# Gate products of an encoder block: reordered first products, splits on GpSimd, earlier tiles for the merge

## The chip, the cores and the metric

The kernel runs on one core of a Trainium2 chip. The metric is device time in microseconds of one execution. The engines are TensorE (PE; its weight loads are PEld), VectorE (DVE), ScalarE (ACT), GpSimd (POOL) and SyncE (SP), which here only issues transfers. Each engine takes its instructions in order.

## The reference

The input is 1024 tokens of width 1024, with 16 meta tokens in front. One layer is computed:

```python
h = h + mixer_block(rms_norm(h, norm_mix), ...)
h = h + swiglu(rms_norm(h, norm_ffn), w_ff_gate, w_ff_up, w_ff_down)
return rms_norm(h, norm_final)[:, N_META:]
# mixer_block: proj = h @ w_in, cut into qa, ka, va, qb, kb, vb, ga, gb
y_a = differential_attention(qa, ka, va, ...)   # 4 heads, every key, two softmaxes subtracted
y_b = windowed_gqa(qb, kb, vb, sink)            # 8 heads, window of 128, meta tokens and sinks
merged = sigmoid(ga) * (y_a @ w_ba) + sigmoid(gb) * (y_b @ w_bb)
return merged @ w_o
```

All of it is float32. The gates ga and gb are 1024 wide each, so their projections are a 1024 x 1024 by 1024 x 2048 product.

## The kernel before

**Precision.** A float32 operand is split in two fp32r tiles, high and low: the high part is a rounded copy, the low part the remainder. A product is three fp32r matmuls: high x high, high x low, low x high. `split` (line 118) makes the copy on ScalarE (line 119) and subtracts on the engine that its last argument names (line 120).

**Stages.** In order: normalisation and projections with the windowed attention (to about 295 us); the differential attention of four heads with the gate products filled in between (to 638 us); the merge, which multiplies both branches with w_bb and w_ba and weighs them with the gates (to 735 us); then the product with w_o and the feed-forward block. TensorE's order is written by hand inside the stages (`tc.manual_schedule`); the order on the other engines and on the queues comes from a planner that simulates a timeline, within the dependences. `tc.issue_after(x)` makes what it holds follow x.

**The gate products.** They use a two by two block scheme with seven products per pair of column blocks instead of eight (the numbers 1 to 7 are names; 1 and 2 give one block, 6 and the sums on it the others). Eight pairs k, each with two blocks of 128 columns. A product (k, p) is 12 matmuls of 128 x 128 by 512, issued in four steps of three; `fill(n)` issues n steps. Its right side (`RIGHT_G`, line 800) is a quarter of the tokens, hT_hi and hT_lo at (d, t): d the half of the width, t the half of the tokens. Some products need sums of token quarters. Those were computed earlier and lie in DRAM as t_d[0] to t_d[3], 2 MB each (high and low); `turn_into(i)` (line 804) loads t_d[i] over a quarter of hT once its last reader is done. `LAST_T` (line 801) names the product after which each is loaded; t_d[2] is loaded with the first head.

**Order.** `first_g` (line 732) holds 24 products: for two pairs at a time (k, 1), (k+1, 1), (k, 2), (k+1, 2), then (k, 6) for all eight pairs. After them come 5, 7, 3, 4 of each pair. The raw weights are read once for 1 and 2 ("f", one tile of 512 KB per pair), again for 6 ("m", two tiles) and again for the rest ("s", two tiles): 40 loads. At most four raw tiles are loaded and not yet freed, two tagged "w" in wpool and two tagged "w2" in gstage (`load_g`, line 745). `weights_g` (line 759) forms the sums of weights on GpSimd and splits the result: the copy on ScalarE, the subtraction on GpSimd. There are four tiles for split operands, so they are made up to four products ahead. The result of (k, 1) goes to DRAM as u_d[k] (line 855), is read back and added to that of (k, 6) (line 862), stored again, and read once more for products 5, 7, 3 and 4.

**Attention and fill.** `load_a` (line 895) loads the queries and keys of a head: for m = 1 and then m = 0, the queries (line 901), and the keys in three transfers (lines 902 and 904). Their tiles have one buffer each, so they wait for the last scores of the head before. Then come 24 gate steps (first head) or 6 (the others), `G_FIRST` and `G_HEAD`, and eight tiles of 128 queries, each of which issues 5 gate steps between its scores (line 934), transposes (line 963) and value products (line 976): 46 steps in a later head, 64 in the first. At the end, `HOLD` = 22 steps follow the last tile.

**The merge.** After the attention, `bops` takes space of the closed apool; the raw y_b is loaded into it. When all gate products are issued, ypool is opened, the gate pools are closed, and ybpool is opened: four tiles yb, split on ScalarE and VectorE (line 1145). The first product of the merge (line 722) reads them. Branch b uses eight weight tiles wbhb, branch a eight wbha, all from six buffers tagged "wh" (`WB_BUFS`, `branch_w` at line 711). The order of branch a keeps up to six of them in use. Gate tiles "gt" have four buffers.

## Time and profile before

| What | us |
|---|---|
| Median of three runs | 1451.18 |
| Lowest and highest run | 1450.22 and 1454.14 |
| Profiled execution | 1455.2 |
| Its span, first to last instruction | 1453.4 |
| TensorE busy in it | 1413.3 (97%) |
| VectorE busy | 914.0 (63%) |
| ScalarE busy | 702.2 (48%) |
| GpSimd busy | 604.3 (42%) |
| Transfers | 229.30 MB, mean 158 GB/s |

In the profile, L848 is line 848 of the kernel before, and names such as `pg` or `wopg` are tiles with their numbers left out: `pg` is a gate product's bank, `wopg` its split weights, `aps` the scores, `apt` the transposes, `at` their copies, `aq` and `ak` queries and keys, `ppa` the merge's products. An arrow `out<-in` gives the tiles written and read; x counts instructions. "Idle before" is the time in which an engine stood still before an instruction, with the one that released it. The granted clock is that of TensorE, 1.00 being full speed. In the slices, the span is cut in 40 equal parts of 36.3 us, and each digit is a share in tenths.

### The profile page before, as it was taken

The page shows a single profiled execution, that of the slowest core. Times are in us where ns is not written, and L with a number is a line of the kernel's source. Part 1 is how long each engine was busy: PE and PEld are TensorE (multiplying, and loading weights), DVE is VectorE, ACT ScalarE, POOL GpSimd, SP SyncE. Part 2 cuts the span into 40 slices and gives each one's busy share as a digit, 9 for nine tenths or more (in the row PEclk, how much of TensorE's full clock was granted, in tenths as well). Part 3 has the DMA queues.
Part 4 walks back from the last instruction along what each step waited for, and adds up shares of the span by engine and source line. Part 5 has one row for each costly group of instructions (what it writes and reads, how often), then busy time and mean ns, then how long its engine had stood idle before and what let it go on. Part 6 is the DMA issues. An engine that isn't in the chain of part 4 may idle for free.

```text
span 1453.4 us, 20758 instructions
## 1 busy us (share of the span) xinstructions
PE 1413.3 (97%) x7183; PEld 1210.1 (83%) x7183; DVE 914.0 (63%) x1584; ACT 702.2 (48%) x1340; POOL 604.3 (42%) x591
## 2 busy tenths in 40 slices
PE   9999999989789999989999999999999999999998
PEld 8998999978678888868888888888888888888886
DVE  6555666527568777734977876654555443787666
ACT  6365556536446565554445654333333333444444
POOL 4157865325367555331422134454454442000442
PEclk9999999999999999999999999999999999999999
DMA  7445564395986545177351633432232322964333
GB/s 228 91 132 160 151 199 140 95 283 184 320 253 196 183 131 183 44 264 229 112 207 58 185 105 117 138 131 102 96 108 102 102 97 99 335 216 138 129 124 145
DMA packets 197258, 229.30 MB, mean 158 GB/s; under 512 B 17480, under 2 KB 129552, under 8 KB 197152
## 3 DMA queue, kind: packets, MB, share of 16 engines
q1 hardware_dynamic: 195232, 225.13, 48.4%
q10 hardware_dynamic: 1920, 2.83, 0.6%
q8 instruction: 57, 0.93, 0.3%
q14 instruction: 49, 0.40, 0.1%
HBM read 154.84 MB, written 66.52 MB: 152 GB/s over the span
## 4 chain that ended last, share of the span: by engine, by line
PE 83%; DMA 6%; DVE 4%; SPq 2%; issue 2%; ACT 1%; POOL 1%; ACTq 0%; DVEq 0%; POOLq 0%
PE pg L1569 29%; PE pd L1673 14%; PE pg L848 6%; PE ppa L722 5%; PE po L1472 4%; PE pp_va L230 3%; PE pp_qa L230 3%; PE aps L934 3%; PE pp_ka L230 3%; PE apy L976 3%; PE bps L397 2%; PE apt L963 2%; PE pp_qb L230 2%; PE po L1480 2%; PE bpy L437 1%
## 5 line engine op out<-in xcount | busy, mean ns | idle before, releaser
L1569 PE MATMUL pg<-t,wop 128*128 128x512 f32 x1056 | 242.4, 389 | 0.0
L1569 PEld LDWEIGHTS pg<-t,wop 128*128 128x128 f32 x1056 | 198.2, 188 | 41.2
L120 POOL TENSOR_TENSOR wop<-wf,wop 128x512 fp32r<-128x512 f32 x114 | 151.3, 1328 | 163.8 <-ACT wop L119 153.6
L1673 PE MATMUL pd<-ob,oa 128*128 128x512 f32 x924 | 209.6, 389 | 0.0
L1673 PEld LDWEIGHTS pd<-ob,oa 128*128 128x128 f32 x924 | 173.4, 188 | 36.0
L1569 PE MATMUL pg<-b,wop 128*128 128x512 f32 x792 | 183.3, 389 | 0.0
L848 PE MATMUL pg<-hT_hi,wopg 128*128 128x512 f32 x448 | 173.7, 408 | 3.0 <-ACT wopg L119 2.4
L1569 PEld LDWEIGHTS pg<-b,wop 128*128 128x128 f32 x792 | 148.4, 188 | 30.7
L119 ACT ACTIVATE wop<-wf 128x512 fp32r<-128x512 f32 x128 | 80.8, 632 | 71.9 <-PE pg L1569 50.8
L120 POOL TENSOR_TENSOR oa<-ra,oa 128x512 fp32r<-128x512 f32 x27 | 34.9, 1294 | 168.6 <-ACT oa L119 167.2
L119 ACT ACTIVATE oa<-ra 128x512 fp32r<-128x512 f32 x77 | 48.7, 632 | 108.5 <-PE pd L1673 47.6
L934 PE MATMUL aps<-ak,aq 128*128 128x352 f32 (+1 forms) x384 | 88.7, 339 | 12.1 <-DMA ak<-ka_d 6.3
L848 PEld LDWEIGHTS pg<-hT_hi,wopg 128*128 128x128 f32 x448 | 86.2, 193 | 16.6 <-ACT wopg L119 2.8
L937 DVE CUSTOM_DVE_ANT_0 as<-aps,dist,far_a 128x704 f32<-128x704 f32 x64 | 60.4, 944 | 59.9 <-PE aps L934 59.8
L945 ACT ACTIVATE as<-as,amn 128x1040 f32<-128x1040 f32 x64 | 74.4, 1162 | 47.3 <-DVE amn L941 47.1
L848 PE MATMUL pg<-hT_lo,wopg 128*128 128x512 f32 x224 | 89.8, 401 | 0.0
L1346 DVE TENSOR_TENSOR s<-wf,wf 128x512 f32<-128x512 f32 x22 | 16.0, 728 | 112.0 <-DMA wf<-in_w_ff_up_dram 70.2
L934 PEld LDWEIGHTS aps<-ak,aq 128*128 128x128 f32 x384 | 65.3, 192 | 22.9 <-DMA ak<-ka_d 6.8
L399 DVE CUSTOM_DVE_ANT_0 bs<-bps,tbx,nsink 128x432 f32<-128x432 f32 (+1 forms) x64 | 38.5, 627 | 56.1 <-PE bps L397 34.6
L409 POOL TENSOR_SCALAR bs<-bs,bdn 128x432 f32<-128x432 f32 (+1 forms) x64 | 36.9, 595 | 78.2 <-DVE bdn L407 49.0
L966 ACT ACTIVATE at<-apt 128x512 fp32r<-128x512 f32 (+1 forms) x96 | 45.5, 484 | 42.1 <-PE apt L963 41.7
L976 PEld LDWEIGHTS apy<-at,av 128*128 128x128 f32 x400 | 56.0, 196 | 4.3
(318 smaller groups left out, 3139.6 us busy)
## 6 DMA issues: line engine op xcount, KB each, us to landing
ra<-aop SPq DMA_DIRECT2D x77, 256.0 KB, 2.6
wf<-in_w_ff_gate_dram SPq DMA_DIRECT2D x25, 512.0 KB, 3.6
wf<-in_w_ff_up_dram SPq DMA_DIRECT2D x25, 512.0 KB, 3.6
aop<-as SPq DMA_DIRECT2D x44, 256.0 KB, 2.1
w_c<-in_w_in_dram SPq DMA_DIRECT2D x17, 512.0 KB, 4.9
aop<-c SPq DMA_DIRECT2D x33, 256.0 KB, 2.0
t_d<-tst SPq DMA_DIRECT2D x16, 512.0 KB, 3.9
g_d<-g SPq DMA_DIRECT2D x32, 256.0 KB, 3.3
```

The costliest lines, as they stand in the source:

```text
L119: high = nc.scalar.activation(hi, src, AF.Copy)
L120: lo_eng.tensor_tensor(lo, src, f32(hi), ALU.subtract)
L230: product = nc.tensor.matmul(ps[:, :n], a[:, c, :], b[:, c, at:at + n], start=(u == 0), stop=(u == 3 * DC - 1))
L722: nc.tensor.matmul(ps, w[:, a, j, :], src(j, b, tk), start=(j == 0 and n == 0), stop=(j == 3 and n == 2))
L848: nc.tensor.matmul(ps, op[:, x, c, :], h[:, 4 * d + c, HALF[t]], start=(p in (1, 6, 7) and c == 0 and i == 0), stop=(p in (2, 6, 3, 4) and ...
L934: nc.tensor.matmul(ps[:, :n], qs[m][:, t * P:(t + 1) * P], ks[m][:, vv, k0:k0 + n], start=(vv == 0), stop=(vv == 1))
L937: nc.vector.tensor_tensor_reduce(s[m][:, 0:2 * n].rearrange("p (a k) -> p a k", a=2), two[:, :, :n], dist[:, u0:u0 + 2 * n].rearrange("p ( ...
L945: nc.scalar.activation(s[m][:, 0:L], s[m][:, 0:L], AF.Exp, bias=mn[:, m, 1:2], scale=-1.0, accum_out=dn[:, 1:2] if m else first_sum)
L976: nc.tensor.matmul(py[:, cols], v[:kp, a, k, :], at_[:kp, k, b, :], start=(k == 0 and j == 0), stop=(k == 8))
L1472: nc.tensor.matmul(sets_o[p][u], oa[:, a, u * P:(u + 1) * P], ob[:, b, :], start=(p in (1, 5) and j == 0 and k == 0), stop=(p in (2, 3) an ...
L1569: nc.tensor.matmul(ps, op[:, x, c, :], b[:, y, c, :], start=(p in (1, 5) and c == 0 and n == 0), stop=(p in (4, 2, 3) and c == 3 and n == ...
L1673: nc.tensor.matmul(ps[u], oa[:, a, u * P:(u + 1) * P], ob[:, b, :], start=(p in (1, 2, 5) and j == 0 and k == 0), stop=(p in (2, 3, 4) and ...
```

## The change

- Pairs 0 to 3 keep their order for products 1 and 2. For k = 4, 5, 6 the order is now (k, 1), (k, 6), (k, 2), (k - 4, 6); then (7, 1), (7, 6), (3, 6), (7, 2). The 24 products stay the same ones. For pairs 4 to 7 both raw tiles are loaded once and serve 1, 6 and 2, so 36 raw loads take the place of 40.
- For pairs 4 to 7 the result of product 1 stays in SBUF until product 6 adds to it; it is neither stored nor read back. For pair 7 it is copied by ScalarE into the bank of product (7, 2), which then adds to it.
- turn_into(0) follows (7, 1), turn_into(1) follows (3, 6), turn_into(3) follows (7, 2); the one that loads in four parts is now 1 and not 3.
- The gates' weights are copied and subtracted on GpSimd; ScalarE has no part in them.
- The queries of a head are loaded after the fourth raw weight.
- "w2", "s" and "ysq" move from gstage into a new pool gwork, inside gstage on the right side.
- ypool is opened before the last gate products; the first two branch weights are split and the first two gate tiles and two yb tiles opened there. When all gate weights are made, gwork is closed and the other two yb tiles are opened.
- WB_BUFS is 3. Branch a's weights 2, 3 and 4 have a tag of their own (wh2, three buffers) in yapool, which is opened when branch b is done.

```diff
 GT_BUFS = 4
-WB_BUFS = 6
+WB_BUFS = 3
 G_HEAD = 6
...
-    def branch_w(p, o, src, nme, raw=None, low=None):
+    def branch_w(p, o, src, nme, raw=None, low=None, tag="wh"):
         w = (raw_tile(f"wbr{nme}_{o}")[:, 0:512] if raw is None else raw).rearrange("p (c n) -> p c n", n=P)
...
             nc.sync.dma_start(w, src[:, o * P:(o + 1) * P].rearrange("(c p) n -> p c n", p=P))
-        wh = p.tile([P, 2, 4, P], F32R, tag="wh", name=f"wbh{nme}_{o}", bufs=WB_BUFS)
+        wh = p.tile([P, 2, 4, P], F32R, tag=tag, name=f"wbh{nme}_{o}", bufs=WB_BUFS)
         split(wh[:, 0], wh[:, 1], w, low or nc.gpsimd)
...
     gstage, close_stage = pool("gstage", "right")
+    gwork, close_gwork = pool("gwork", "right")
     apool, close_apool = pool("apool")
...
     G_COLS = [C_GB + 2 * k * P for k in range(4)] + [C_GA + 2 * k * P for k in range(4)]
-    first_g = [(k, p) for i in (0, 2, 4, 6) for p in (1, 2) for k in (i, i + 1)] + [(k, 6) for k in range(8)]
+    first_g = [(k, p) for i in (0, 2) for p in (1, 2) for k in (i, i + 1)]
+    first_g += [kp for k in (4, 5, 6) for kp in ((k, 1), (k, 6), (k, 2), (k - 4, 6))] + [(7, 1), (7, 6), (3, 6), (7, 2)]
     order_g = first_g + [(k, p) for k in range(8) for p in (5, 7, 3, 4)]
...
         else:
-            uses_g.append({1: [("f", k, 0)], 2: [], 6: [("m", k, 0), ("m", k, 1)]}[p])
+            uses_g.append({1: [("f", k, 0)], 2: [], 6: [("f", k, 1)] if k >= 4 else [("m", k, 0), ("m", k, 1)]}[p])
     loads_g = [u for us in uses_g for u in us]
...
             kind, k, i = key = loads_g[n_loaded[0]]
-            p, tag = ((wpool, "w"), (gstage, "w2"))[n_loaded[0] // 2 % 2]
+            p, tag = ((wpool, "w"), (gwork, "w2"))[n_loaded[0] // 2 % 2]
             n_loaded[0] += 1
...
                     after.enter_context(tc.issue_after(keys_a[0].ins))
-                nc.sync.dma_start(w, w_in[:, col:col + P].rearrange("(c p) n -> p c n", p=P))
-
-    sums_g, keys_a = {}, []
+                raws_g.append(nc.sync.dma_start(w, w_in[:, col:col + P].rearrange("(c p) n -> p c n", p=P)))
+
+    sums_g, keys_a, raws_g = {}, [], []
...
         nm = f"{k}_{p}"
-        kind = "s" if n >= n_first else "m" if p == 6 else "f"
+        kind = "s" if n >= n_first else "m" if p == 6 and k < 4 else "f"
         wa, wb = raw_g[kind, k, 0], raw_g.get((kind, k, 1))
...
             src = a12
-            n_freed[0] += 1
+            n_freed[0] += 1 if k < 4 else 2 if k < 7 else 4
         elif p == 6:
...
             src = a21
-            n_freed[0] += 2
+            if k < 3:
+                n_freed[0] += 2
         elif p == 5:
-            src = sums_g[k] = gstage.tile([P, 4, P], F32, tag="s", name=f"s1g_{k}", bufs=1)
+            src = sums_g[k] = gwork.tile([P, 4, P], F32, tag="s", name=f"s1g_{k}", bufs=1)
             tt(src, a21, a22, ALU.add)
...
         op = ops_g[n] = wpool.tile([P, 2, 4, P], F32R, tag=("wh", "wl")[n % 2], name=f"wopg_{nm}", bufs=W_BUFS)
-        split(op[:, 0], op[:, 1], src, nc.gpsimd)
+        nc.gpsimd.tensor_copy(op[:, 0], src)
+        tt(op[:, 1], src, f32(op[:, 0]), ALU.subtract)
...
     RIGHT_G = {1: (0, 0), 6: (0, 1), 2: (1, 0), 5: (0, 0), 7: (0, 1), 3: (1, 1), 4: (1, 0)}
-    LAST_T = {(7, 1): 0, (7, 2): 3, (7, 6): 1}
+    LAST_T = {(7, 1): (0,), (3, 6): (1,), (7, 2): (3,)}
     INTO_T = {2: (0, 1), 0: (0, 0), 1: (0, 1), 3: (1, 0)}
...
         d, t = INTO_T[i]
-        for c in (range(4) if i == 3 else (slice(0, 4),)):
+        for c in (range(4) if i == 1 else (slice(0, 4),)):
             for hl, h in enumerate((hT_hi, hT_lo)):
...
             ensure_g(n + 1)
-            for k_next in [0] * (n in (n_first - 9, n_first - 2)) + [k + 1] * (p == 6 and k < 7):
+            k_next = {(7, 6): 0}.get((k, p), k - 4 if p == 1 and k >= 4 else k + 1 if p == 7 and k < 7 else None)
+            if k_next is not None:
                 kept[k_next] = kept_g(f"u_{k_next}")
                 nc.sync.dma_start(kept[k_next], u_d[k_next])
+            if (k, p) == (3, 6):
+                banks[1, 7] = bank(psum2, f"pp{(n + 1) % 2}", "pg_7_2", 1)
+                nc.scalar.copy(banks[1, 7], kept.pop("p1"))
             if n == n_first - 1 or (p == 4 and k < 7):
...
             if p in (1, 2):
-                banks[1, k] = banks.get((1, k), banks[1])
+                banks[1, k] = banks.get((1, k), banks.get(1))
             ps = banks[1, k] if p in (1, 2) else banks[{3: 5, 4: 7}.get(p, p)]
...
                         nc.scalar.copy(p1, ps)
-                        nc.sync.dma_start(u_d[k], p1)
+                        if k < 4:
+                            nc.sync.dma_start(u_d[k], p1)
+                        else:
+                            kept[k if k < 7 else "p1"] = p1
                     elif p == 2:
...
                     elif p == 6:
-                        u = kept.pop(k)
-                        add(u, ps, u, ALU.add)
+                        p1 = kept.pop(k) if k < 7 else kept["p1"]
+                        u = p1 if k < 7 else kept_g("u_7")
+                        add(u, ps, p1, ALU.add)
                         nc.sync.dma_start(u_d[k], u)
...
                         store(st, 2 * k + (p == 4), int(p == 3))
-                    if (k, p) in LAST_T:
-                        turn_into(LAST_T[k, p])
+                    for i in LAST_T.get((k, p), ()):
+                        turn_into(i)
                     if p == 4:
                         del kept[k]
-                    if p == 7 and k < 7:
-                        kept[k + 1] = kept_g(f"u_{k + 1}")
-                        nc.sync.dma_start(kept[k + 1], u_d[k + 1])
                 yield
...
             k = ks[m] = p.tile([P, 2, L], F32R, tag=f"k{m}", name=f"ak{h}_{m}")
-            nc.sync.dma_start(f32(q), qa_d[h][m])
+            with tc.issue_after(raws_g[3].ins):
+                nc.sync.dma_start(f32(q), qa_d[h][m])
             nc.sync.dma_start(f32(k)[:, 0, :], ka_d[h][m])
...
         nm = f"{h}_{c}"
-        ysq = gstage.tile([P, 512], F32, tag="ysq", name=f"ysq_{nm}", bufs=1)
+        ysq = gwork.tile([P, 512], F32, tag="ysq", name=f"ysq_{nm}", bufs=1)
         nc.scalar.activation(ysq, py, AF.Square)
...
             nc.sync.dma_start((a12, w11)[h][:, j], yb_d[j][:, h * 512:h * 512 + 512])
+    ypool, close_ypool = pool("ypool")
+    first_w = [branch_w(ypool, o, w_bb, "b", raw) for o, raw in enumerate((a11[:, 2], asum[:, 0]))]
+
+    def gate_tile(name):
+        return ypool.tile([P, 512], F32, tag="gt", name=name, bufs=GT_BUFS)
+
+    first_gt = [gate_tile(f"gt_0_{o}") for o in range(2)]
+    yb_t = []
+
+    def split_yb(p, j0):
+        for j in (j0, j0 + 1):
+            yb_t.append(p.tile([P, 2, S], F32R, name=f"yb{j}"))
+        for h in range(2):
+            cols = slice(h * 512, h * 512 + 512)
+            for k in (j0, j0 + 1):
+                split(yb_t[k][:, 0, cols], yb_t[k][:, 1, cols], (a12, w11)[h][:, k], nc.vector)
+
+    ybpool, close_yb = pool("ybpool")
+    split_yb(ybpool, 0)
     while tail:
...
         fill(1)
+    while n_made[0] < len(order_g):
+        fill(1)
+    close_gwork()
+    ybpool2, close_yb2 = pool("ybpool2")
+    split_yb(ybpool2, 2)
     order_pe.__exit__(None, None, None)
     fill(1000)
-    ypool, close_ypool = pool("ypool")
     close_psum2()
...
     w12, w21 = (wopool.tile([P, 4, 512], F32, name=f"w{n}") for n in ("12", "21"))
-    ybpool, close_yb = pool("ybpool")
-
-    first_w = [branch_w(ypool, o, w_bb, "b", raw) for o, raw in enumerate((a11[:, 2], asum[:, 0]))]
-
-    yb_t = []
-    for j in range(4):
-        yb_t.append(ybpool.tile([P, 2, S], F32R, name=f"yb{j}"))
-        if j % 2:
-            for h in range(2):
-                cols = slice(h * 512, h * 512 + 512)
-                for k in (j - 1, j):
-                    split(yb_t[k][:, 0, cols], yb_t[k][:, 1, cols], (a12, w11)[h][:, k], nc.vector)
-
     def yb(j, b, tk):
...
         tk = slice(half * 512, half * 512 + 512)
-        gt = ypool.tile([P, 512], F32, tag="gt", name=f"gt_{i}_{o}_{half}", bufs=GT_BUFS)
+        gt = first_gt.pop(0) if first_gt else gate_tile(f"gt_{i}_{o}_{half}")
         nc.sync.dma_start(gt, g_d[8 * i + o][:, tk])
...
             split_ya(0, j)
+    close_yb2()
     close_yb()
...
         if o_next not in ws_a:
-            ws_a[o_next] = branch_w(ypool, o_next, w_ba, "a", None, nc.vector)
+            ws_a[o_next] = branch_w(*((yapool, o_next, w_ba, "a", None, nc.vector, "wh2") if 2 <= o_next < 5 else
+                                      (ypool, o_next, w_ba, "a", None, nc.vector)))
         nc.gpsimd.tensor_tensor(merged(o, half), gt, merged(o, half), ALU.add)
```

## The prediction

> **What bounds the kernel now.** I read the page's busy shares first, then the slices, then the waits of TensorE, then the single gaps in order of time, and last the queues behind them.
>
> ```profile
> span 1453.4 us, 20758 instructions
> PE 1413.3 (97%) x7183; PEld 1210.1 (83%) x7183; DVE 914.0 (63%) x1584; ACT 702.2 (48%) x1340; POOL 604.3 (42%) x591
> ...
> POOL 4157865325367555331422134454454442000442
> PEclk9999999999999999999999999999999999999999
> DMA  7445564395986545177351633432232322964333
> ```
>
> TensorE is busy for 1413.3 of 1453.4 us. The change removes no matmul (24 first products and 32 later ones, as before), so it can win only where TensorE stands still or runs slowly. Those places are in the waits of TensorE between 285 and 660 us, the gate products with the differential attention, and the start of the merge (in us: total, times, longest):
>
> ```profile
> PE aps L934 <- DMA ak<-ka_d: 6.3, 2, 4.8
> PE ppa L722 <- ACT yb L119: 6.2, 1, 6.2
> PE apt L963 <- DVE at L967: 4.7, 5, 2.0
> PE apt L963 <- DVE as L951: 3.2, 4, 1.3
> PE aps L934 <- issue: 2.7, 1, 2.7
> PE pg L848 <- ACT wopg L119: 2.4, 1, 2.4
> PE aps L934 <- DVE at L967: 1.4, 1, 1.4
> ```
>
> The same gaps in order of time (start, duration, and in brackets the idle time before):
>
> ```profile
> 295.53 0.39 PE L848 MATMUL pg<-hT_hi,wopg 128*128 128x512 f32 x1
> ...
> 306.21 0.39 PE L848 MATMUL pg<-hT_hi,wopg 128*128 128x512 f32 x1
> 309.01 0.80 PE L848 MATMUL pg<-hT_hi,wopg 128*128 128x512 f32 x1 [2.41 <-ACT wopg L119]
> ...
> 394.24 1.25 PE L934 MATMUL aps<-ak,aq 128*128 128x352 f32 x3 [4.79 <-DMA ak<-ka_d]
> ...
> 434.13 0.63 PE L963 MATMUL apt<-ident,as 128*128 128x128 f32 x4 [2.00 <-DVE at L967]
> ...
> 644.49 20.78 PE L722 MATMUL ppa<-yb,wbhb 128*128 128x512 f32 x78 [6.17 <-ACT yb L119]
> ```
>
> Behind each long gap the granted clock drops, which the table by stretch shows (us; busy time and count of PE, PEld, DVE, ACT, POOL; clock; DMA share; GB/s):
>
> ```profile
> 309.00:316.00 7.00, 6.86 (x16) 5.03 (x17) 0.00 (x0) 2.70 (x5) 4.98 (x4) 0.53 1.03 290
> 395.00:400.00 5.00, 4.64 (x23) 3.98 (x22) 2.39 (x6) 1.58 (x3) 0.00 (x0) 0.75 1.06 276
> 404.00:409.00 5.00, 5.00 (x24) 4.50 (x23) 2.98 (x7) 1.85 (x3) 3.18 (x4) 0.66 0.86 270
> 434.00:440.00 6.00, 5.87 (x28) 5.51 (x29) 5.76 (x10) 2.94 (x7) 6.00 (x6) 0.72 0.76 230
> 644.50:650.70 6.20, 6.19 (x15) 4.52 (x16) 6.20 (x12) 6.18 (x12) 0.46 (x1) 0.55 1.02 336
> 691.00:731.00 40.00, 39.80 (x176) 32.65 (x175) 39.17 (x48) 16.75 (x29) 20.18 (x12) 1.00 0.39 133
> ```
>
> A gap costs its idle time plus the busy time behind it times one minus the clock. Start of the gates: 2.4 + 6.86 x 0.47 = 5.6 us. Second head: 2.7 + 4.8 + 1.4 + 1.5 = 10.4, plus 4.64 x 0.25 + 5.00 x 0.34 = 2.9, is 13.3 us. At 434: 2.0 + 5.87 x 0.28 = 3.6 us. Merge: 6.2 + 6.19 x 0.45 = 9.0 us. Together 31.5 us: that is what the change can win, beside about 6 us of short waits on VectorE (the rest of 4.7, and 3.2).
>
> [...]
>
> **The change part by part.**
>
> *The second head's keys.* What SP issues there:
>
> ```profile
> 376.08 2.96 SPq L901 DMA_DIRECT2D aq<-qa_d  x1
> ...
> 379.61 0.38 SPq L813 DMA_DIRECT2D hT_hi<-t_d  x1
> ...
> 389.98 0.32 SPq L813 DMA_DIRECT2D hT_lo<-t_d  x1
> ...
> 391.64 0.32 SPq L901 DMA_DIRECT2D aq<-qa_d  x1
> ```
>
> The token sums of turn_into(0) and turn_into(3), 2 MB each, stand before and between the queries and keys, and the second query load goes out 15.6 us after the first, behind the last of the sums, which wait for their product on TensorE. The change fires turn_into(0) after (7, 1), turn_into(1) after (3, 6) and turn_into(3) after (7, 2), now entries 20, 22 and 23 of the order. The first head takes 24 + 8 x 5 = 64 quarter-product steps, or 16 products, so all three fall inside the second head. Also gone by then: four of 40 weight loads of 512 KB, and four stores and four loads of 256 KB (first products of pairs 4 to 7 stay on chip): 4 MB of traffic. How a head starts without sums in the way is shown by the third, which waited 0 us for keys:
>
> ```profile
> 465.00 0.32 SPq L901 DMA_DIRECT2D aq<-qa_d  x1
> ...
> 475.88 0.80 PE L934 MATMUL aps<-ak,aq 128*128 128x352 f32 x4
> ```
>
> First load to first score is 10.9 us there; in the second head TensorE stopped at 394.24 - 4.79 - 0.4 - 2.7 = 386.3, 10.3 us after 376.08, so there was as much lead. So nearly all of 13.3 us goes; I leave 1.3 (the `at` wait has another cause) and take 12.0, bounds 4 (only the 15.6 us hole in the loads closes, DMA stays full) to 13.3.
>
> *The start.* Queries and keys now follow the fourth raw weight (raws_g[3]). Now they go the other way:
>
> ```profile
> 299.17 0.55 SPq L901 DMA_DIRECT2D aq<-qa_d  x1
> ...
> 300.80 1.36 SPq L755 DMA_DIRECT2D wg_f<-in_w_in_dram  x2
> ```
>
> With the weights first, 1 MB at the 290 GB/s of that stretch lands near 299.2 + 3.6 + 2 = 305, before TensorE runs out at 306.4; the 5.6 us goes. What is late next: a step is three matmuls, 3 x (306.21 - 295.53) / 47 = 0.68 us, so 24 steps end at 311.8 and the other scores of the first tile come some 2.4 us later, at 314.2. Weights, queries and keys are 4.2 MB, 14.5 us at 290 GB/s, so the last key lands near 316. I let 2.4 us return: gain 3.2, bounds 0 to 5.6.
>
> *Gate weights on GpSimd alone.* 56 copies leave ScalarE and come to GpSimd. The rows (ns min/median/max):
>
> ```profile
> L927 POOL COPY far_m<-dist x32: 441/452/1505, 299.3 to 595.2; 128x320 f32<-128x320 f32 x32
> L952 POOL COPY as<-as x32: 199/209/220, 327.1 to 616.5; 128x32 f32<-128x32 f32 x32
> L120 POOL TENSOR_TENSOR wopg<-wg_s,wopg x24: 1271/1289/2353, 441.1 to 629.5; 128x512 fp32r<-128x512 f32 x24
> L951 DVE SCALAR_TENSOR_TENSOR as<-as,adn,as x32: 1285/1302/2386, 325.7 to 615.0; 128x1040 f32<-128x1040 f32 x32
> 432.14 0.63 ACT L119 ACTIVATE wopg<-s1g 128x512 fp32r<-128x512 f32 x1 [5.05 <-POOL s1g L781]
> ```
>
> A copy 512 wide isn't shown: bounds 0.45 (320 wide) and 1.29 (the two-input form of that width). From 32 to 320 columns it grows by 0.84 ns a column, so I take 0.61 us, nearest to the lower row. 56 x 0.61 = 34 us over 340 us is one tenth more in GpSimd slices that stand at two to seven tenths: hidden, since weights are made four products ahead and an operand takes 0.61 + 1.29 = 1.9 us against 2.7 us of a product with nothing between; a sum for product 3 or 6 adds 2.6, covered by the attention between products. If that cover is gone (1.29 a copy) a product with two sums costs 4 x 1.29 = 5.2 us against (465.00 - 376.08) / 11.5 = 7.7 us a product in the mixed stage, where a head has 46 steps or 11.5 products: still hidden. What it wins is the row at 432.14: ScalarE, in order, stood 5.05 us for a GpSimd sum with the `at` copies of the attention behind it, and the gap at 434 followed. That wait moves into GpSimd's own order: 3.6 us, bounds 0 to 3.6.
>
> The row that speaks against it is L951, two operands in SBUF: median 1.30, up to 2.39 us. One tenth more GpSimd work meets some three more of 32, and waits of up to a copy reach the short waits on VectorE: I charge 1.3 us, bounds 0 to 4. [...]
>
> *The merge's start.* The eight ScalarE halves of yb run at 643.83, all after the last gate product (ends 638.3), and TensorE waits for them:
>
> ```profile
> 643.83 4.25 ACT L119 ACTIVATE yb<-m 128x512 fp32r<-128x512 f32 x8
> ```
>
> Their data came much earlier, as the chain in order of time says (start, duration):
>
> ```profile
> 626.77 6.58 DMA m<-yb_d
> ```
>
> In the code their tiles lie in a pool opened after the gate pools close. Now ypool and the first two yb tiles lie in space that apool leaves, the other two where gwork was, free once the last weight is made, up to four products of 2.7 us or 11 us before the end. Data at 633.4 and the last four halves, 2.1 us on ScalarE and as much on VectorE behind it, fit before 638.3. What is late next: PSUM's first bank and the gates' last evacuation, under 1 us. Gain 8.0, bounds 2 (four splits after the end) to 9.0.
>
> *Fewer branch-weight buffers.* Six to three, and three more (wh2) where yb lay, so branch a's weights 2 to 4 can't be split before branch b ends: three VectorE splits move into the stretch where VectorE is busy 39.17 of 40 us. There one came just in time:
>
> ```profile
> 712.79 0.68 DVE L120 TENSOR_TENSOR wbha<-wbra,wbha 128x512 fp32r<-128x512 f32 x1
> ```
>
> 3 x 0.68 = 2.0 us of lateness there would stop TensorE for up to that, with a half clock behind it 5 us; VectorE has caught up before the next stage. I charge 1.5, bounds 0 to 5.
>
> *The rest.* Prefetches of u, seeding (7, 2) by a ScalarE copy (0.6 us, a product earlier), and the raw slots held longer: covered by one product each, bounds -1 to 1, taken as 0. The sums read later have 8 to 12 steps of 1.9 us, 15 to 23 us, before product 7, 4 or 5 reads them, against 7.2 us for 2 MB at 290 GB/s; behind SP's wait for their product stand weight loads made four products ahead: 0.
>
> **Sum.** 12.0 + 3.2 + 3.6 + 8.0 - 1.3 - 1.5 = 24.0 us. The profiled execution took 1455.2 us, 4.0 over the median of the runs: 1431.2 there, 1427 as a median.
>
> **The rivals.**
>
> *Keys still late* (0.13): SP's order puts the doubled raw loads of pairs 4 to 6 before the second head's keys. For it: DMA is full whatever moves there (share 1.06); against: 4 MB less, sums gone. The hole closes for 4 us, which the raw loads take again: 1427 + 12 = 1439.
>
> *Merge gap stays* (0.10): ScalarE or VectorE, in order, waits for another load ahead of the yb halves. For it: today they stand behind other splits; against: their data are in at 633.4. 1427 + 7 = 1434.
>
> *GpSimd blocks VectorE* (0.05): every one of the 32 L951 waits for a whole copy, 32 x 0.61 = 19.5 us on TensorE's path, 1446. For it: the 2.39 us of the row; against: the median of 1.30. [...]
>
> *Sums late* (0.08), the other side: SP's in-order queue holds turn_into(0), (1), (3) until their products end, three times 2 MB inside the second head, beside weights and u. If products 5, 7 and 4 of pair 0 each wait the full 7.2 us plus about 2.2 of half clock, 28 us is lost, and the gain of 24.0 is overtaken from three full waits on: 1427 + 28 = 1455. For it: SP waits today at 389.98; against: 15 to 23 us of lead.
>
> *All of it* (0.08): the gaps close whole and the short waits shrink with ScalarE's relief: 31.5 + 4 won, 1455.2 - 35.5 - 4.0 = 1416.
>
> **How the numbers follow.** My forecast has 0.56 (the rivals' chances taken from 1), its own range 1420 to 1434. The range 1419 to 1442 holds it and the first two rivals, and leaves out the last three, 0.21, less what of them falls short of their full price. A measurement of this kernel can tell 0.3%, 4.4 us: below 1446.8 is faster. That takes in all but the late sums, most of the blocking, and a tenth of the keys: faster 0.87, same 0.04, slower 0.09.
>
> **What would show it.** The wait of L934 for ak gone at the second head, with the reads of t_d behind it; no half clock near 310, 434 or the merge; ScalarE's L119 on wopg gone, GpSimd copies near 0.61 us; yb halves before the last gate product; wbha in the 40 us stretch later by about 2 us. I would be wrong if L848 waits for t_d or GpSimd, or if the keys still wait.

## The result, and the profile after

The changed kernel took 1431.88 us (median of 4 runs, 1430.95 to 1433.72) against 1450.7 us of the kernel before on the same chip (4 runs, 1449.28 to 1454.14): a ratio of 0.9868, 95% interval 0.9848 to 0.9889. Another series gave 1434.52 us and 0.9865 (0.9849 to 0.9882). So it is faster by about 19 us, and the predicted 1427 us was 5 us too low. The profiled execution took 1431.73 us, and its span is 23.4 us shorter than that of the profile before, which lay 4 us above its median.

The page of the changed kernel, its span and busy shares, then the slices of GpSimd, the clock and the transfers:

```profile
span 1430.0 us, 20687 instructions
PE 1406.6 (98%) x7183; PEld 1206.1 (84%) x7183; DVE 917.9 (64%) x1584; ACT 673.3 (47%) x1285; POOL 639.7 (45%) x647
...
POOL 4156865437568666332503045455444552000442
PEclk9999999999999999999999999999999999999999
DMA  8445564387687354197331724423332332954434
```

ScalarE lost 29 us of work and GpSimd gained 35: the 56 copies. TensorE's busy time fell by 6.7 us with the same 7183 matmuls, as the mean granted clock rose from 0.990 to 0.996. What TensorE waited for between 285 and 660 us (total, times, longest):

```profile
PE pg L856 <- POOL wopg L797: 5.9, 3, 3.3
PE aps L944 <- DVE amn L947: 2.5, 8, 0.4
PE aps L944 <- DMA ak<-ka_d: 2.4, 2, 1.8
PE apt L973 <- DVE as L961: 1.8, 2, 1.3
PE apt L973 <- DVE at L977: 1.4, 2, 0.7
PE ppa L722 <- ACT g L886: 0.2, 1, 0.2
```

The wait of 6.2 us at the merge and the 4.8 us for the second head's keys are gone. (The 2.4 us for keys here are the first head's.) At the top stands a wait of which the kernel before had 0.5 us: gate matmuls (L856) for the low half that GpSimd subtracts (L797). TensorE's single gaps in order of time (start, duration, in brackets the idle time before):

```profile
305.41 0.72 PE L856 MATMUL pg<-hT_hi,wopg 128*128 128x512 f32 x2 [1.04 <-POOL wopg L797]
313.64 0.40 PE L944 MATMUL aps<-ak,aq 128*128 128x352 f32 x1 [0.61 <-DMA ak<-ka_d]
315.88 1.02 PE L944 MATMUL aps<-ak,aq 128*128 128x352 f32 x3 [1.83 <-DMA ak<-ka_d]
324.20 0.66 PE L973 MATMUL apt<-ident,as 128*128 128x128 f32 x4 [1.32 <-DVE as L961]
330.51 0.80 PE L856 MATMUL pg<-hT_hi,wopg 128*128 128x512 f32 x1 [3.33 <-POOL wopg L797]
340.47 0.50 PE L856 MATMUL pg<-hT_hi,wopg 128*128 128x512 f32 x1 [1.54 <-POOL wopg L797]
...
389.13 0.80 PE L944 MATMUL aps<-ak,aq 128*128 128x352 f32 x4
...
623.75 16.62 PE L722 MATMUL ppa<-yb,wbhb 128*128 128x512 f32 x72 [0.23 <-ACT g L886]
```

The second head (389.13) starts without a gap and the merge (623.75) with 0.23 us, but the two gaps of 3.33 and 1.54 us stand where no step of the prediction had put a loss. The stretches around them (busy time and count of PE, PEld, DVE, ACT, POOL; clock; DMA share; GB/s):

```profile
316.00:320.00 4.00, 4.00 (x13) 3.42 (x14) 1.61 (x5) 0.12 (x1) 0.45 (x1) 0.57 1.05 396
...
328.00:332.00 4.00, 1.49 (x6) 1.30 (x7) 1.53 (x2) 1.74 (x3) 4.00 (x5) 0.72 1.09 347
332.00:336.00 4.00, 4.00 (x13) 3.31 (x13) 2.78 (x5) 0.88 (x2) 4.00 (x4) 0.50 0.70 254
...
667.40:707.40 40.00, 40.00 (x177) 32.97 (x176) 38.52 (x47) 16.49 (x29) 19.80 (x12) 1.00 0.50 154
```

In the stretch that holds most of the gap of 3.33 us transfers stand at 1.09; in the 4 us behind it TensorE runs at 0.50 and transfers fall to 0.70. GpSimd is busy throughout both. Why the low half is late, the rows of the changed kernel say: first two raw loads on SP's queue and what stands between them, then GpSimd:

```profile
314.35 0.39 SPq L757 DMA_DIRECT2D wg_f<-in_w_in_dram  x1
315.80 5.13 SPq L864 DMA_DIRECT2D u_d<-p  x1
321.03 0.38 SPq L757 DMA_DIRECT2D wg_f<-in_w_in_dram  x1
...
325.78 1.17 POOL L796 CAST wopg<-wg_f 128x512 fp32r<-128x512 f32 x2 [5.92 <-DMA wg_f<-in_w_in_dram]
327.97 1.26 POOL L777 TENSOR_TENSOR wg_f<-wg_f 128x512 f32<-128x512 f32 x1 [1.02 <-DMA wg_f<-in_w_in_dram]
329.19 1.27 POOL L797 TENSOR_TENSOR wopg<-wg_f,wopg 128x512 fp32r<-128x512 f32 x1
```

The first raw of pair 4 is asked for at 314.35 and used at 325.78, 11.4 us later, behind a full queue of transfers (a share of 1.05 from 310 to 320 us and of 1.06 from 320 to 330). GpSimd then makes the copies, which are the high halves, of (4, 1) and (4, 2), and next in its order stands the sum for (4, 6), which waits 1.02 us for the second raw. Only after it comes the subtraction for (4, 1), for which TensorE stands. The second raw went out late because SP stood 5.13 us on a store of u whose product wasn't done. That stand is not new: the kernel before has one of 5.22 us at 317.34. New is what hangs on the raw behind it, two sums on GpSimd.

A table from both traces and from those of the experiments below says where each stage gained. Gate product n starts with its first matmul (the gates have 12 each, so product 8 starts with the 97th), "gates' end" is the start of the last gate matmul; all lengths in us. In the names, "p_only" and so on are the runs of the next section.

| kernel | span start to product 8 | 8 to 12 | 12 to 16 | 16 to 24 | 24 to gates' end | gates' end to branch a | branch a to end |
|---|---|---|---|---|---|---|---|
| before | 329.25 | 25.31 | 27.40 | 65.95 | 190.03 | 53.01 | 762.47 |
| p_only | 328.72 | 27.12 | 26.27 | 64.41 | 189.81 | 52.80 | 762.91 |
| s_only | 325.58 | 25.00 | 27.44 | 61.46 | 190.34 | 52.29 | 762.80 |
| m_only | 328.67 | 25.31 | 27.49 | 60.77 | 192.76 | 43.79 | 762.35 |
| after | 326.45 | 32.21 | 26.28 | 47.93 | 190.27 | 44.27 | 762.55 |
| after_again | 329.19 | 32.53 | 26.30 | 48.93 | 191.66 | 43.79 | 761.99 |
| no_p | 328.31 | 30.61 | 26.28 | 52.59 | 189.98 | 43.79 | 762.17 |
| no_raws_first | 326.43 | 33.00 | 26.29 | 49.12 | 191.03 | 43.75 | 761.92 |
| sub_first | 327.57 | 32.78 | 26.29 | 47.98 | 190.31 | 44.00 | 761.99 |
| t2_late | 330.56 | 27.01 | 27.41 | 51.38 | 190.31 | 44.53 | 761.94 |
| t2_sub_first | 327.00 | 28.19 | 26.31 | 50.48 | 190.22 | 43.89 | 761.95 |
| t2_sub_again | 330.07 | 28.69 | 26.30 | 51.04 | 189.82 | 44.78 | 761.89 |
| t2_sub_hyb | 327.36 | 26.08 | 26.30 | 51.33 | 191.46 | 44.30 | 761.96 |
| no_t2 | 329.62 | 25.09 | 27.26 | 48.00 | 189.62 | 44.59 | 761.98 |

Between after and before: 18.0 us are won from product 16 to 24 (the second head), 8.7 at the merge, 6.9 are lost from product 8 to 12. Up to product 8 the three kernels that send the first queries ahead of the raw weights (before, p_only, s_only) lie at 325.6 to 329.3 and the eleven that send the raws first at 326.4 to 330.6: the profiles of one order lie as far apart as the two orders do, so the 2.8 us there can be put down to no part of the change. A row is one execution, and the profile before was one of the slower ones; after and after_again, the same kernel twice, differ by up to 2.7 us in one stage.

### The profile page after: what moved, and what is told of

Same layout as the page of the kernel before. It is cut to its first block, busy times and chain, and to the rows that moved or that the text cites. A ratio compares the mean times of both kernels' runs of the same rounds, so it can differ in the third digit from the quotient of the medians.

```text
span 1430.0 us, 20687 instructions
## 1 busy us (share of the span) xinstructions
PE 1406.6 (98%) x7183; PEld 1206.1 (84%) x7183; DVE 917.9 (64%) x1584; ACT 673.3 (47%) x1285; POOL 639.7 (45%) x647
## 3 DMA queue, kind: packets, MB, share of 16 engines
q1 hardware_dynamic: 189920, 220.94, 48.9%
## 4 chain that ended last, share of the span: by engine, by line
PE 88%; DVE 4%; DMA 4%; ACT 2%; issue 1%; SPq 1%; POOL 1%; ACTq 0%; DVEq 0%; POOLq 0%
PE pg L1591 29%; PE pd L1695 14%; PE ppa L722 6%; PE pg L856 6%; PE po L1494 4%; PE pp_va L230 3%; PE pp_qb L230 3%; PE aps L944 3%; PE pp_qa L230 3%; PE pp_ka L230 3%; PE apy L986 3%; PE bps L397 2%; PE po L1502 2%; DMA wg_f<-in_w_in_dram 1%; PE bpy L437 1%; PE bpt L432 1%
## 5 line engine op out<-in xcount | busy, mean ns | idle before, releaser
L856 PE MATMUL pg<-hT_hi,wopg 128*128 128x512 f32 x448 | 172.6, 405 | 6.1 <-POOL wopg L797 5.9
L856 PEld LDWEIGHTS pg<-hT_hi,wopg 128*128 128x128 f32 x448 | 85.6, 191 | 19.8 <-POOL wopg L797 7.2
L856 PE MATMUL pg<-hT_lo,wopg 128*128 128x512 f32 x224 | 89.1, 398 | 0.0
L976 ACT ACTIVATE at<-apt 128x512 fp32r<-128x512 f32 (+1 forms) x96 | 45.3, 484 | 52.0 <-PE apt L973 51.9
```

The source lines that it names most:

```text
L856: nc.tensor.matmul(ps, op[:, x, c, :], h[:, 4 * d + c, HALF[t]], start=(p in (1, 6, 7) and c == 0 and i == 0), stop=(p in (2, 6, 3, 4) and ...
```

## The experiments

**The parts one at a time.** Three kernels put one part each into the kernel before, and a fourth takes one out of the changed kernel. All four ran on one chip, with the kernel before at 1452.35 us (19 runs).

p_only: the copies go to GpSimd, nothing else.

```diff
-        split(op[:, 0], op[:, 1], src, nc.gpsimd)
+        nc.gpsimd.tensor_copy(op[:, 0], src)
+        tt(op[:, 1], src, f32(op[:, 0]), ALU.subtract)
```

> Kernel before with the gates' weights copied on GpSimd instead of ScalarE, nothing else. Theory 1 (ScalarE's in-order wait for a GpSimd sum made the gap at 434): that gap, 2.0 us and 1.6 us of clock, goes, the starts of the gates and of the second head stay; 1.5 to 3.6 us faster than before. Theory 2 (what stalled the changed kernel at 330 to 340 us, 4.9 us of gaps and about as much clock, comes from the copies on GpSimd as such): a gap of TensorE before L848 on a GpSimd subtraction turns up here too and the kernel is 3 to 8 us slower than before. Theory 3 (it comes only with the doubled raw loads of the new order): no such gap here.

Measured: 1454.73 us (10 runs), ratio 1.0016 (0.9998 to 1.0034). TensorE's waits between 285 and 660 us in its trace:

```profile
PE ppa L722 <- ACT yb L119: 5.9, 1, 5.9
PE pg L849 <- POOL wopg L794: 5.2, 3, 3.1
PE aps L935 <- DMA hT_lo<-t_d: 5.0, 1, 5.0
PE aps L935 <- issue: 4.4, 1, 4.4
```

Alone it wins nothing: where ScalarE's copy is gone, three waits for GpSimd's subtraction, 5.2 us, have come. That is theory 2's wait, but the time is only some 2 us longer, and the interval includes 1. The gap at 434 has not gone for good either: 1.92 us of such a wait stand at 441.5.

s_only: the token sums are asked for later in the program, at entries 20, 22 and 23 of the old order.

```diff
-    LAST_T = {(7, 1): 0, (7, 2): 3, (7, 6): 1}
+    LAST_T = {(4, 6): 0, (6, 6): 3, (7, 6): 1}
```

> Kernel before with the token sums loaded after entries 20, 22 and 23 of the old order ((4, 6), (6, 6) and (7, 6)), nothing else; all raw loads and the traffic of u stay. Theory 1 (the sums' place in SP's queue and in DMA made the second head wait for its keys): the waits for ak go, 9 to 13 us faster than before. Theory 2 (the amount of traffic there, 4 MB more than in the changed kernel, made it): half of the wait or more stays, 0 to 5 us faster. Theory 3 (sums read too late): TensorE waits for t_d at products 5, 7 or 4 of pair 0.

Measured: 1448.86 us (10 runs), ratio 0.9976 (0.9963 to 0.9988). The stage of the second head is 4.5 us shorter, of the changed kernel's 18.0, and a wait for keys stays:

```profile
PE aps L934 <- DMA ak<-ka_d: 7.9, 4, 3.6
```

But the run did not take the sums out of the second head's start. The planner, which orders the queues within the dependences, sent eight of the ten transfers of t_d[0] and t_d[3] among or behind its queries and keys again, at 380.88 to 397.85; only the two query loads stand closer, 6.7 us apart instead of 15.6. Rows of s_only:

```profile
375.61 0.53 SPq L901 DMA_DIRECT2D aq<-qa_d  x1
...
380.88 1.37 SPq L813 DMA_DIRECT2D hT_hi<-t_d  x1
382.35 1.02 SPq L901 DMA_DIRECT2D aq<-qa_d  x1
...
387.87 0.32 SPq L813 DMA_DIRECT2D hT_lo<-t_d  x1
```

In the changed kernel the first of these sums goes out behind them all:

```profile
413.53 0.38 SPq L817 DMA_DIRECT2D hT_lo<-t_d  x1
```

So in s_only the hole closed by 9 us while the transfers stayed, and it is 3.5 us faster by the ratio: near the lower bound of the prediction's first step (4 us, "only the 15.6 us hole in the loads closes, DMA stays full"). What the sums' absence is worth, the run does not show. Nor can the 4.5 us of the stage be put down to the hole alone: this trace has no gap at 434 (2.00 us in the kernel before, with a clock of 0.72 behind it), and m_only, below, is 5.2 us shorter there with the sums where they were.

m_only: the new places for ypool, the yb tiles and three of branch a's weights.

```diff
-WB_BUFS = 6
+WB_BUFS = 3
...
+    ybpool, close_yb = pool("ybpool")
+    split_yb(ybpool, 0)
...
+    close_gwork()
+    ybpool2, close_yb2 = pool("ybpool2")
+    split_yb(ybpool2, 2)
```

> Changed kernel with the gate order, the loads and the copies on ScalarE put back as before: the merge's part alone (gwork, ypool and yb earlier, three and three weight buffers). Theory 1: the gap of 6.2 us before the first L722 and its half clock go, 8 to 9 us faster than before, and the buffers cost nothing. Theory 2: part of that is given back in branch a for weights 2 to 4 or product 6 of the order: 4 to 7 us faster.

Measured: 1445.8 us (4 runs), ratio 0.9952 (0.9937 to 0.9968). From the gates' end to branch a it takes 43.79 us instead of 53.01: 9.2 us, and nothing comes back in branch a (762.35 against 762.47), as theory 1 has it; but the medians differ by 6.6 us, which is theory 2's number. Its second head is also 5.2 us shorter. It has no gap at 434 either; what else shortens it stays open. The planner also sends the raws ahead of the first queries here.

no_p: the changed kernel with the copies on ScalarE again.

```diff
-        nc.gpsimd.tensor_copy(op[:, 0], src)
-        tt(op[:, 1], src, f32(op[:, 0]), ALU.subtract)
+        split(op[:, 0], op[:, 1], src, nc.gpsimd)
```

> Changed kernel with the gates' weights copied on ScalarE again. Theory 1 (the GpSimd copies cost what the changed kernel lost at 330 to 340 us, about 8 us, and win 3.6 us near 420): 2 to 6 us faster than the changed kernel, 1426 to 1430, with no wait of L848 for a subtraction there. Theory 2 (the late raw load costs it, whoever copies): the gap at 330 stays and ScalarE's waits return, 1432 to 1437.

Measured: 1435.05 us (4 runs), ratio 0.9879 (0.9865 to 0.9894); the changed kernel's interval overlaps it. The loss from product 8 to 12 stays (30.61 against 25.31), so the engine that copies is not its cause. It shows elsewhere: the gap at 330 is 0.47 us, and at 338 TensorE waits 1.71 us for ScalarE's copy and 0.62 us for a subtraction. The second head takes 52.59 us against 47.93 and 48.93 in the two profiles of the changed kernel; its trace has a gap of 1.66 us at 421.9 on a copy of the attention (L976), where the changed kernel has none over 0.4 us, and 2.2 us of waits for keys. So the copies on GpSimd seem to help here, by about 4 us in the profiles and 1.6 us by the ratios, whose intervals overlap.

The three parts together give 1.0016 x 0.9976 x 0.9952 = 0.9944, 8 us; the whole gives 0.9868, 19 us. The other 11 us need the new order of products, which lets the sums go out behind the second head's start and has four weight reads and eight transfers of 256 KB fewer, or the parts in company.

**Where the 7 us between products 8 and 12 come from.** From product 8 to 11 the old order makes (4, 1), (5, 1), (4, 2) and (5, 2) from two raw loads; the new one makes (4, 1), (4, 6), (4, 2) and (0, 6) from four, with four sums on GpSimd. Two theories: transfers, which are full there (a share of 1.05 over 300 to 332 us) and bring the raws late; or GpSimd, its order and its load. T2, 2 MB, is the largest transfer that can be moved in that stretch. t2_late puts it behind the sixth raw load.

```diff
-                        after.enter_context(tc.issue_after(keys_a[0].ins))
+                        after.enter_context(tc.issue_after(raws_g[5].ins))
...
+            if n == 5:
+                turn_into(2)
...
-        if not h:
-            turn_into(2)
```

> The changed kernel, with the store and load of T2 (2 MB, ahead of head 1) issued after the sixth gate operand's raw load instead of after the first key block, so that both raw loads of the next pair go out ahead of it. Theory A (the 4.1 us that the changed kernel loses by product 12 come from raw loads landing late in saturated transfers): the 3.33 us gap before GpSimd's subtraction shrinks under 1 us, product 12 starts 3 to 7 us earlier than in the changed kernel, and so does the end: 1425 to 1429 us. Theory B (the transfers are late whatever their order, because the queue has too many bytes): the raws land earlier but T2 lands late, head 1 waits for it, and the time is within 1 us of the changed kernel.

Measured: 1432.41 us (4 runs, 1428.74 to 1435.02), ratio 0.9861 (0.9838 to 0.9884), beside 1451.95 us of the kernel before (7 runs). The stage falls from 32.2 to 27.0 us, as theory A has it, but the end does not move: theory B's number. Its second head is 3.5 us longer than in the first profile of the changed kernel and 2.5 us longer than in the second, with waits for keys of 1.83 us together (after_again has one of 1.16 us):

```profile
393.67 0.40 PE L944 MATMUL aps<-ak,aq 128*128 128x352 f32 x1 [0.47 <-DMA ak<-ka_d]
395.43 0.72 PE L944 MATMUL aps<-ak,aq 128*128 128x352 f32 x3 [1.36 <-DMA ak<-ka_d]
```

sub_first: GpSimd's sum issued only behind the subtraction ahead of it.

```diff
-            tt(a21, a21, a22, ALU.add)
+            with tc.issue_after(subs_g[-1].ins):
+                tt(a21, a21, a22, ALU.add)
...
-        tt(op[:, 1], src, f32(op[:, 0]), ALU.subtract)
+        subs_g.append(tt(op[:, 1], src, f32(op[:, 0]), ALU.subtract))
```

> The changed kernel, with GpSimd's first sum of the next pair issued only after the subtraction of the operand before it. Theory A (the gap of 3.33 us is GpSimd's order: a sum that waits for a load stands ahead of a subtraction whose operand is there): the gap before that subtraction goes, product 12 starts 2 to 4 us earlier, and the end is 2 to 4 us earlier, 1428 to 1430 us. Theory B (the load itself is what is late, and the order only chooses where it shows): the wait moves to the next operand's subtraction, and the time is within 1 us of the changed kernel.

Measured: 1433.63 us (4 runs), ratio 0.9873 (0.9857 to 0.9888). The first gap shrinks and the next one grows:

```profile
329.36 0.50 PE L857 MATMUL pg<-hT_hi,wopg 128*128 128x512 f32 x1 [1.05 <-POOL wopg L798]
...
341.36 0.80 PE L857 MATMUL pg<-hT_hi,wopg 128*128 128x512 f32 x1 [4.07 <-POOL wopg L798]
```

The stage stays at 32.78 us: GpSimd's order only chooses where the wait shows (theory B).

t2_sub_first: both edits.

> Both: T2's transfer behind the sixth raw load and the first sum behind the subtraction ahead of it. If the late load and GpSimd's order each cost a part of their own, the end is 4 to 8 us earlier than in the changed kernel (1424 to 1428 us); if they are one and the same loss, it is no better than the better one of the two alone, within 1 us.

Measured: 1428.55 us (4 runs, 1426.51 to 1430.92), ratio 0.9837 (0.9818 to 0.9855). In its trace no gap over 0.9 us on GpSimd's subtraction is left; the second head is 2.6 and 1.6 us longer than the changed kernel's two.

no_t2 leaves T2's transfer out, to price it.

```diff
-        if not h:
-            turn_into(2)
```

> The changed kernel without the 2 MB transfer of T2 into the normalised input's tiles ahead of head 1 (the products that read T2 read what was there before it). Theory A (the loss between product 8 and product 12 is the number of bytes asked for at 300 to 332 us): the share of the transfers falls under 1 from about 325 us on, the raw loads land 3 to 6 us earlier, and product 12 starts 4 to 7 us earlier than in the changed kernel. Theory B (it is GpSimd's order and load): product 12 starts within 2 us of the changed kernel.

Measured: 1429.49 us (4 runs), ratio 0.9835 (0.9817 to 0.9853), in the series with 1453.58 us of the kernel before (7 runs). The stage takes 25.09 us, as before the change, with all of GpSimd's copies, sums and subtractions; GpSimd's sum for (4, 6) starts 4.3 us earlier and waits 0.22 us for its raw:

```profile
323.68 1.30 POOL L777 TENSOR_TENSOR wg_f<-wg_f 128x512 f32<-128x512 f32 x1 [0.22 <-DMA wg_f<-in_w_in_dram]
```

and the table by stretch shows room in the transfers from 325 us on (0.81 at 330 to 340 in the changed kernel):

```profile
325.00:330.00 5.00, 2.66 (x16) 2.35 (x16) 3.67 (x7) 2.29 (x4) 4.87 (x5) 1.00 0.94 315
330.00:340.00 10.00, 8.88 (x51) 7.17 (x50) 7.02 (x18) 5.89 (x12) 8.59 (x11) 1.00 0.73 212
```

This settles the place of the loss: 2 MB too many in the stretch that needs four raw loads instead of two. In the four kernels that move T2 the second head takes 50.5 to 51.4 us, against 47.9 and 48.9 in the changed kernel and 48.00 with T2 missing. In t2_late part of that is a wait for keys; in t2_sub_first, where the keys wait 0.30 us, it isn't one wait that the trace names, and what ties it to T2 stays open.

**The start.** no_raws_first takes away the rule that the first head's query block waits for the fourth raw load.

```diff
-            with tc.issue_after(raws_g[3].ins):
-                nc.sync.dma_start(f32(q), qa_d[h][m])
+            nc.sync.dma_start(f32(q), qa_d[h][m])
```

> The changed kernel without the rule that the first head's query block waits for the fourth raw load. Theory A (the stretch up to product 8 is bound by transfers whatever their order, so that the 4 us gained at the first head's scores are lost again by product 8): the first score comes 2 to 5 us later but product 8 within 1 us, and the time is within 1 us of the changed kernel. Theory B (the start gain of 3.2 us that the prediction put on it is kept): 3 to 5 us slower, 1435 to 1437 us.

Measured: 1433.62 us (4 runs), ratio 0.9871 (0.9855 to 0.9888), against 0.9868 and 0.9865 of the changed kernel. The first score comes at 311.1, against 310.5, and product 8 at 326.43, against 326.45. But this does not decide between the theories, for SP's order has not changed:

```profile
297.31 1.34 SPq L757 DMA_DIRECT2D wg_f<-in_w_in_dram  x2
298.69 1.15 SPq L910 DMA_DIRECT2D aq<-qa_d  x1
```

The planner sends both raws ahead of the first queries without the rule, and it does so in m_only, which has no such rule either. So the rule is worth nothing here, and what the order is worth has to be read from the traces that differ in it. From the gates' first matmul to the first score the three with the queries first take 22.4 (before), 23.0 (p_only) and 19.6 us (s_only), the eleven with the raws first 17.3 to 18.4. From the gates' first matmul to product 8 the three take 32.4 to 34.3 us and the eleven 32.7 to 36.6. The first scores do come earlier with the raws first, and by product 8 the lead is gone, which is what theory A says of the stretch.

**A better version.** Three kernels once more, in the series of no_t2, with the changed kernel as the measure.

> The changed kernel once more, as the measure for the three beside it: 1431 to 1434 us. If the 2.7 us by which its profile was ahead at the gates' first matmul (292.85 against 295.53) belong to that one execution, they come out differently here; if they belong to the change, they stay.

Measured: 1434.52 us (4 runs), ratio 0.9865. The gates' first matmul is at 293.50 here, and at 293.0 to 295.1 in the eleven other profiles beside the first of the changed kernel (292.85) and of the kernel before (295.53): spread of executions.

> T2's transfer behind the sixth raw load and GpSimd's first sum behind the subtraction ahead of it, once more. If its 3 us on the changed kernel are real, it is 2 to 5 us faster than it here (ratio to the kernel before by 0.0015 to 0.0035 lower); if they were the spread of two series of runs, within 1 us.

Measured: 1431.5 us (4 runs, 1426.18 to 1434.37), ratio 0.9846 (0.9821 to 0.9872).

t2_sub_hyb puts the copies of the first 24 operands back on ScalarE.

```diff
-        nc.gpsimd.tensor_copy(op[:, 0], src)
+        (nc.scalar.copy if n < n_first else nc.gpsimd.tensor_copy)(op[:, 0], src)
```

> As the one before, with the copies of the operands taken while the first four pairs are made put back on ScalarE (the later ones stay on GpSimd). If GpSimd's load (9 us of 10 busy at 330 to 350) is what is late there, 1 to 4 us faster than with all copies on GpSimd; if the loads are what is late, the same within 1 us, or up to 2 us slower where ScalarE's exponentials wait behind the copies.

Measured: 1431.12 us (4 runs), ratio 0.9848 (0.9833 to 0.9863). It takes 26.08 us from product 8 to 12, 2.6 less than its neighbour, but ends no earlier. The version with T2 and the sum moved was ahead of the changed kernel twice (once against its ratio from another series), by 0.0031 and 0.0019 of the kernel before's time (4.5 and 2.8 us); the intervals overlap each time, so about 3 us is likely and not shown.

## Why the prediction was right, and where it was not

The sign, the range and two of the main mechanisms held; the time came out 5 us over, since a gain was counted that does not last and a loss was put at nothing.

- **Second head's keys, 12.0 us, and the gap at 434, 3.6 us.** Together 15.6; the stage from product 16 to 24 is 18.0 us shorter than in the profile before, and 12.8 to 16.5 shorter than in the three kernels with one part. The size was right, as far as single profiles tell. Of the reason, the traces agree with the step: the sums go out behind 413 us and the second head's keys are in time. But s_only, which was to show it, left most of the sums where they were, so no run separates the sums' part from that of the 4 MB fewer. The gap at 434 was no steady property: s_only and m_only, with the copies on ScalarE, have no gap over 0.6 us between 405 and 450 us, while no_p, with the same copies, has one of 1.66 us at 421.9.
- **The start, 3.2 us.** The mechanism held and the size was wrong. With the raws first the wait of 2.4 us on ScalarE's copy goes (1.04 us on GpSimd's subtraction are left), and the first score comes 4.7 us sooner behind the gates' first matmul (17.7 against 22.4). The 2 us that the step added to the 3.6 us of both raws have no row beside them; sent from 296.44 on, the second was in at 302.83, 6.4 us later and not 5.6. "I let 2.4 us return" foretold the wait for the first head's keys, and it came: 0.61 and 1.83 us in the rows above. But the step left out the half clock behind that wait, which it had counted behind the gap it closed: 0.57 over 316 to 320 us, some 1.7 us more. From the first score to product 8 the changed kernel takes 15.9 us, the kernel before 11.3: 4.6 us return, and nothing of the gain is left. The half clock that the step counted as won was not certain either. In s_only TensorE stops at the same place, and the clock stays at 1.00 from 306.3 to 312.0:

```profile
306.34 0.50 PE L848 MATMUL pg<-hT_hi,wopg 128*128 128x512 f32 x1 [2.08 <-ACT wopg L119]
```

- **Merge's start, 8.0 us.** Right: 8.7, and 9.2 alone. The eight halves on ScalarE ran ahead of the last gate matmul (623.14), as the step had it:

```profile
L119 ACT ACTIVATE yb<-m x8: 617/632/636, 614.1 to 620.7; 128x512 fp32r<-128x512 f32 x8
```

- **Branch a's weights later, a cost of 1.5 us.** It did not come: the 40 us stretch has TensorE busy for 40.00 of them, with VectorE at 38.52. The lower bound, 0, was the value.
- **GpSimd and VectorE, a cost of 1.3 us.** It came on VectorE and did not reach TensorE. The copies took what was estimated (0.61 us) in all but five of 56, and VectorE's instruction with two operands has nearly the median and the longest time that it had (1302 and 2386 ns):

```profile
L796 POOL CAST wopg<-wg_f x20: 600/611/617, 276.6 to 411.5; 128x512 fp32r<-128x512 f32 x20
...
L961 DVE SCALAR_TENSOR_TENSOR as<-as,adn,as x32: 1285/1303/2418, 322.8 to 600.0; 128x1040 f32<-128x1040 f32 x32
```

  But medians hide the meetings. One of them, VectorE's row and then GpSimd's:

```profile
565.61 2.41 DVE L961 SCALAR_TENSOR_TENSOR as<-as,adn,as 128x1040 f32<-128x1040 f32 x1
...
565.63 1.30 POOL L797 TENSOR_TENSOR wopg<-s1g,wopg 128x512 fp32r<-128x512 f32 x1
```

  Nine of the 32 met no GpSimd instruction and took 1285 to 1303 ns; the 23 that met one took 1547 ns on average. The five slow copies, 1421 to 1632 ns, all ran beside this instruction. The 2.41 us above are 0.19 us less than its median of 1.30 and GpSimd's 1.30 together, but ten of the 23 took no longer than 1303 ns, so a meeting alone did not lengthen it. The charge of 1.3 us was an estimate from the row's longest time, and no run shows it as a cost of time; what the traces show is that in sum the 32 took 46.7 us before and 47.3 and 48.1 in the two profiles after, 0.6 to 1.4 us more; TensorE's waits for them fell from 3.2 to 1.8 us.
- **The rest, 0.** Wrong by 7 us, the largest miss. "Covered by one product each" was said of the prefetch of u, the seeding and the raw slots; the raw loads themselves were never costed, though the rival of the late keys names "the doubled raw loads of pairs 4 to 6". The row for it stood in the table by stretch of before: a DMA share of 1.03 at 309 to 316 us. Four loads of 512 KB where two had been, in a stretch without room, is 1 MB, by estimate 3.6 us of lateness at the 290 GB/s of that row, and the half clock behind the gap (0.50 for 4 us) gives about 2 more. The sums read later, the rival with a price of 28 us, cost nothing.

Against the 24.0 us predicted the terms add up so: start -3.2, the loss -6.9, the two costs that did not reach TensorE +2.8, second head +2.4, merge +0.7. That leaves 19.8 us. The two profiles differ by 23.4, of which 2.8 lie before product 8 and 1.1 between products 12 and 16, where 26.3 and 27.4 us both occur in kernels with and without the new order; the medians differ by 18.8.

Of the rivals, the second head's keys came in time (in after_again 1.16 us late), the merge gap closed, GpSimd held VectorE up in some meetings without TensorE waiting longer, and the sums were not late. The mark that the prediction named as a sign of being wrong, that the gate matmuls (L848 there) would wait for GpSimd, did appear: 5.9 us.

## What to carry to other kernels

Where transfers stand at a full share over a stretch (1.05 over 300 to 332 us here), a new order of work has to be costed in bytes asked for within that stretch, and a transfer moved out of it has to be followed to the next full stretch: here moving 2 MB won 5.2 us in one stage, and the second head after it was 2.5 to 3.5 us longer, though no run shows that the one made the other. A gap closed early in such a stretch has to be followed to its end: here the first score came 4.7 us sooner, and product 8 came no sooner. And an edit that is to test an order has to be checked in the trace: where a planner decides, it may leave the order much as it was, as in s_only and no_raws_first. A wait for a load has to be followed past the instruction at which it shows: in sub_first another order on GpSimd cut the first gap from 3.33 to 1.05 us, lengthened the next from 1.54 to 4.07 us, and left the time where it was (a ratio of 0.9873 against 0.9868).

## What was not expected of the hardware

- A 128x512 copy from f32 to fp32r on GpSimd takes 611 ns (median), less than half of the two-operand form of that width (1288 ns) and as much as a split of that width on ScalarE (632 ns in the row of the yb halves).
- In the stretch from 300 to 345 us a raw load of 512 KB into wg_f took between 4.0 and 11.3 us from issue to landing, median 5.6:

```profile
DMA to landing us min/median/max: 4.0/5.6/11.3
```

- The clock was 0.50 at 332 to 336 us, after a gap of 3.33 us, and at 340 to 350 us, after one of 1.54 us, it was 1.00. The length of a gap alone did not decide: behind 1.83 us at 315.88 it was 0.57 and behind 2.41 us at 309.01 in the kernel before 0.53, but behind 2.08 us at 306.34 in s_only 1.00.
- VectorE's instruction with two operands in SBUF (L961) took up to 2.42 us instead of 1.30 beside a GpSimd one, and GpSimd's copy up to 1.63 us instead of 0.61 beside it.
